# 42 instead of 32 tokens in the second gathered set of a PEER layer

## The chip, the core and the metric

The kernel runs on one core of a Trainium2 chip. The metric is device time in microseconds; the kernel before took 2982.0 us (median of three runs, 2977.97 to 2984.56). "MB" and "GB/s" are decimal.

## What is computed

One decoder layer in float32 on 512 tokens of width 2048: RMSNorm, one input projection, two mixers side by side (a chunked gMLP and an mLSTM), an output projection, and then the part that this change touches, a product-key expert retrieval (PEER), followed by a last RMSNorm.

```python
qp = (xc @ peer_wq).reshape(128, 8, 128)          # per token 8 heads
s1, s2 = q1 . peer_k1, q2 . peer_k2               # 128 scores each
v1, i1 = top_k(s1, 16);  v2, i2 = top_k(s2, 16)
cand = v1[:, None] + v2[None, :]                  # 256 candidates
sv, pos = top_k(cand, 16);  eidx = i1*128 + i2 at pos
gate = softmax(sv)
u_sel, v_sel = peer_u[eidx], peer_v[eidx]         # (128 tokens, 8, 16, 2048)
act = gelu(einsum("td,thkd->thk", xc, u_sel))
y   = einsum("thk,thkd->td", gate * act, v_sel)
```

Each token picks 128 of 16384 experts (8 heads, 16 each); a row of `peer_u` or `peer_v` is 8 KB, a table 134 MB.

## The kernel before

**Two ways for the experts.** The tokens are shared between two ways that run at the same time. *Gathered* tokens (the first `TG` = 160): an indirect DMA on GpSimd's queue (L553) fetches 128 rows of a table, one expert row for each partition, 1 MB at a time; VectorE multiplies a `peer_u` row by the token's input and sums (L580), or adds a gated `peer_v` row to an accumulator (L594). The first set is tokens 0 to 127, one token per partition, 128 fetches for each table. The second set is `G2` = 32 tokens, of which each stands on `S2` = 4 partitions with 32 experts each, so it takes 32 fetches for each table, and at the end a small matmul (`pick`, L885 to L890) adds up the four partial sums. Its input rows `h21` must stand four times on the partitions; L578 reads them from DRAM with an outermost dimension of 4 copies and a step of 0.

*Dense* tokens (`TD` = 352): TensorE computes every expert for them. All of `peer_u` and `peer_v` is streamed in 1 MB loads on SyncE's queue (`raw`, L91), each split into a high and a low float32r half (`split`: ScalarE L73 makes `whi`, VectorE L74 makes `wlo`), and each product is three matmuls (`mm3`, L102 to L104). One *piece* is half a load: 24 matmuls of 352 columns. 256 pieces make the `pu` loop (L742) and 256 the `pv` loop (L835). Between the two, expert activations go to DRAM as `Ad` (L758), and the gates, scattered by one-hot matmuls (`combine`, L668: `pwb`), as `Wd`, in blocks of 32 tokens. `product(g)` (L709) loads both for eight experts (`At`, `Wt`), multiplies them on VectorE (L721) and splits the result (`C`), which is the moving operand of the `pv` matmuls.

**What sets the order.** Python generators interleave the streams, and a scheduler then orders each engine's queue. After each piece `gather_step` (L627) issues `left/slots` gathers, (2·128 + 2·32)/466 = 0.69 for each piece, at a share of 0.45 around the change of loops (once `product(0)` has begun, and in the first 12 pieces of `pv`); a gather is tied to the matmuls of the pieces just before it (`pace`, L555), so that TensorE's pace sets the gathers' pace. Routing (`route`, 102 steps, taken as 1.15 each) and `combine` (88 steps) are spread over the pieces of `pu` by the rate at L764, and `product(0)` begins when they have ended. Weight loads run three pieces ahead. All of VectorE's work stands in one queue in order: splits, gathered rows, routing, PSUM evacuations (L853) and products, so a VectorE instruction that waits holds up the splits behind it, and with them TensorE.

**The end.** `settle` (L808) transposes the dense result back, adds the residual rows `xf` (loaded at L895, one DMA for each of the pieces of tokens in `toks`: 96, 128 and 128 rows), normalizes, and stores `out` in six DMAs (L832), two for each of the three.

Of the kernel before, what the change touches and what calls it, by code (L numbers as in the profile page):

```python
# [39 lines left out]
def layer(ctx, tc, a, out, dbg=None):  # L40
# [440 lines left out]
    def route(t, heads=range(8), nb=4):  # L481
        s = slice(t * P, (t + 1) * P)
        for h0 in range(heads[0], heads[-1] + 1, nb):
# [54 lines left out]
            if t == 1:  # L538
                for q in range(S2):
                    c = q * G2 - r.start  # L540
                    if 0 <= c < nb * TOPK:
                        d = slice(q * G2, (q + 1) * G2)
                        nc.sync.dma_start(eidx2[d, :], ei[0:G2, c:c + G2])
                        nc.sync.dma_start(gate2[d, :], sels[t][0:G2, 2, d])
                        done[1] += 1
# [119 lines left out]
    NB = TD // 32  # L665
    Wd = tc.dram_tile([NB, P, P, 32], F32, name="Wd")

    def combine():  # L668
# [3 lines left out]
        with ExitStack() as wx:  # L672
# [3 lines left out]
            for t in range(1, NT):  # L676
# [5 lines left out]
                for blk in range(G2 // 32 if t == 1 else 0, 4):  # L682
                    wst = wp.tile([P, P, 32], F32, name="wst", bufs=2)
                    for f in range(8):
                        pw = bank("sm", f"pwb{t}_{blk}_{f}")
                        c0 = blk * 32 + f * 4
                        four = [P, 4, P]
                        o1 = wp.tile(four, F32, name="o1", bufs=2)
                        o2 = wp.tile(four, F32, name="o2", bufs=2)
                        nc.vector.tensor_tensor(o1, io[:, None, :].to_broadcast(four),  # L690
                                                sT[:, 0, c0:c0 + 4, None].to_broadcast(four), op=ALU.is_equal)
                        nc.vector.tensor_tensor(o2, io[:, None, :].to_broadcast(four),
                                                sT[:, 1, c0:c0 + 4, None].to_broadcast(four), op=ALU.is_equal)
                        for i in range(4):
                            nc.scalar.activation(o1[:, i, :], o1[:, i, :], AF.Copy, scale=sT[:, 2, c0 + i:c0 + i + 1])
                            nc.tensor.matmul(pw[:, i * P:(i + 1) * P], o2[:, i, :], o1[:, i, :], start=True, stop=True)  # L696
                        nc.scalar.activation(wst[:, :, f * 4:f * 4 + 4].rearrange("p i t -> p t i"),
                                             pw.rearrange("p (t i) -> p t i", t=4), AF.Copy)
                        yield
                    nc.gpsimd.dma_start(Wd[(t - 1) * 4 + blk - G2 // 32], wst)  # L700
# [258 lines left out]
```

## Time and profile before

| | us |
|---|---|
| median of 3 runs | 2982.0 |
| the profiled execution | 2980.37 |
| its span (first to last instruction) | 2978.7 |
| TensorE busy (matmul) | 2893.9 (97%) |
| VectorE busy | 2195.9 (74%) |
| ScalarE busy | 1131.2 (38%) |
| GpSimd busy | 543.1 (18%) |
| granted TensorE clock, mean | 0.988 |
| DMA | 800.76 MB, mean 269 GB/s |

An average over the whole span hides the stages: the first 818 us (the mixers) move little data, and from 900 us on weights, gathered rows and products share the DMA engines. So the rows below are read by stage. "PE" is TensorE, "DVE" VectorE, "ACT" ScalarE, "POOL" GpSimd, "SP" SyncE; a "q" behind an engine's name is its queue. A matmul's duration in a row is not its price: the matmuls overlap, and the distance from start to start counts.

### The profile page before, as it was taken

The numbers are of one execution on the slowest core, as the hardware profiler recorded it, in microseconds if no ns is written. First come the engines' busy times: TensorE is split into PE (matmuls) and PEld (weight loads), VectorE is DVE, ScalarE is ACT, GpSimd is POOL, SyncE is SP. The second block draws the span as 40 slices with busy tenths as digits, with TensorE's granted clock in tenths as the row PEclk, the third lists the DMA queues.
The fourth block names the chain that finished last, engine by engine and source line by source line (L and its number), as shares of the span: only waits on it lengthen the run. The fifth ranks groups of instructions, "written<-read, shape, count | busy, mean of one in ns | idle before, by whom it ended". The sixth has DMA issues, their size and how long they took to land.

```text
span 2978.7 us, 41459 instructions
## 1 busy us (share of the span) xinstructions
PE 2893.9 (97%) x16709; PEld 2727.6 (92%) x16709; DVE 2195.9 (74%) x3026; ACT 1131.2 (38%) x1634; POOL 543.1 (18%) x363
## 2 busy tenths in 40 slices
PE   9999999999989999999999999979999999999997
PEld 7888888887889999999999999979999999999997
DVE  5634333324598999998888886668988989889955
ACT  5322244323243333334676675322323333232233
POOL 0000000000022313322122221013323332223200
PEclk9999999999999999999999999989999999999999
DMA  6223222324379888989889889889999999999853
GB/s 241 85 85 121 85 92 92 106 93 178 112 285 360 312 319 307 330 328 347 305 342 367 332 330 356 315 260 357 370 365 360 361 368 355 362 367 352 344 198 108
DMA packets 147029, 800.76 MB, mean 269 GB/s; under 512 B 15108, under 2 KB 37684, under 8 KB 68596
## 3 DMA queue, kind: packets, MB, share of 16 engines
q1 hardware_dynamic: 87604, 401.68, 36.7%
q0 software_dynamic: 50016, 373.36, 33.3%
q10 hardware_dynamic: 9216, 23.07, 2.0%
q8 instruction: 131, 2.15, 0.3%
q14 instruction: 62, 0.51, 0.0%
HBM read 741.39 MB, written 56.62 MB: 268 GB/s over the span
## 4 chain that ended last, share of the span: by engine, by line
PE 84%; DVE 7%; DMA 5%; issue 2%; ACT 1%; SPq 0%; ACTq 0%; DVEq 0%; POOLq 0%
PE pv L104 9%; PE pu L104 9%; PE pu L102 9%; PE pu L103 9%; PE pv L102 9%; PE pv L103 9%; PE pn L102 4%; PE pn L103 4%; PE pn L104 4%; PE pwb L696 3%; DMA raw<-in_v 2%; DVE wlo L74 2%; PE po L102 2%; PE po L104 2%; PE po L103 2%
## 5 line engine op out<-in xcount | busy, mean ns | idle before, releaser
L73 ACT ACTIVATE whi<-raw 128x1024 fp32r<-128x1024 f32 x642 | 664.7, 1056 | 1395.5 <-DMA raw<-in_v 435.2
L74 DVE TENSOR_TENSOR wlo<-raw,whi 128x1024 fp32r<-128x1024 f32 x642 | 773.1, 1217 | 494.8 <-ACT whi L73 491.0
L102 PE MATMUL pu<-Th,whi 128*128 128x352 f32 x2048 | 671.4, 328 | 13.7 <-ACT whi L73 13.7
L102 PE MATMUL pv<-C,whi 128*128 128x352 f32 x2048 | 663.0, 324 | 18.4 <-ACT whi L73 18.3
L104 PE MATMUL pu<-Th,wlo 128*128 128x352 f32 x2048 | 664.8, 326 | 9.6 <-DVE wlo L74 9.5
L103 PE MATMUL pu<-Tl,whi 128*128 128x352 f32 x2048 | 664.0, 324 | 0.0
L103 PE MATMUL pv<-C,whi 128*128 128x352 f32 x2048 | 661.9, 324 | 0.0
L104 PE MATMUL pv<-C,wlo 128*128 128x352 f32 x2048 | 607.2, 325 | 13.1 <-DVE wlo L74 13.1
L553 POOL DMA_INDIRECT g<-in_peer_v,eidx x160 | 274.7, 1717 | 745.3 <-PE pv L104 303.1
L102 PEld LDWEIGHTS pv<-C,whi 128*128 128x128 f32 x2048 | 386.5, 189 | 21.0 <-ACT whi L73 19.9
L102 PEld LDWEIGHTS pu<-Th,whi 128*128 128x128 f32 x2048 | 388.0, 189 | 16.3 <-ACT whi L73 15.7
L104 PEld LDWEIGHTS pu<-Th,wlo 128*128 128x128 f32 x2048 | 387.1, 189 | 11.4 <-DVE wlo L74 11.0
L104 PEld LDWEIGHTS pv<-C,wlo 128*128 128x128 f32 x2048 | 377.1, 189 | 18.8 <-DVE wlo L74 17.9
L580 DVE CUSTOM_DVE_ANT_0 g<-h,g 128x2048 f32<-128x2048 f32 x160 | 364.5, 2281 | 39.2 <-DMA g<-in_peer_u,eidx 39.1
L553 POOL DMA_INDIRECT g<-in_peer_u,eidx x160 | 248.1, 1550 | 793.3 <-PE pu L104 268.9
L594 DVE SCALAR_TENSOR_TENSOR acc<-g,gate,acc 128x2048 f32<-128x2048 f32 x160 | 375.2, 2345 | 18.8 <-DMA g<-in_peer_v,eidx 18.3
L103 PEld LDWEIGHTS pu<-Tl,whi 128*128 128x128 f32 x2048 | 387.7, 189 | 0.1
L103 PEld LDWEIGHTS pv<-C,whi 128*128 128x128 f32 x2048 | 386.2, 189 | 0.8 <-issue 0.8
L103 PE MATMUL pn<-wlo,Th 128*128 128x512 f32 x512 | 204.9, 400 | 0.0
L104 PE MATMUL pn<-whi,Tl 128*128 128x512 f32 x512 | 203.7, 398 | 0.0
L102 PE MATMUL pn<-whi,Th 128*128 128x512 f32 x512 | 182.9, 399 | 0.0
L853 DVE TENSOR_TENSOR top<-pv,top 128x352 f32<-128x352 f32 x240 | 119.5, 517 | 71.6 <-PE pv L104 70.5
(269 smaller groups left out, 2841.8 us busy)
## 6 DMA issues: line engine op xcount, KB each, us to landing
raw<-in_u SPq DMA_DIRECT2D x128, 1024.0 KB, 7.3
raw<-in_v SPq DMA_DIRECT2D x128, 1024.0 KB, 7.4
raw<-in_w_in SPq DMA_DIRECT2D x80, 512.0 KB, 3.3
Ad<-ast ACTq DMA_DIRECT2D x64, 352.0 KB, 6.9
Wd<-wst POOLq DMA_DIRECT2D x11, 2048.0 KB, 13.0
At<-Ad SPq DMA_DIRECT2D x32, 704.0 KB, 8.3
raw<-in_w_out SPq DMA_DIRECT2D x32, 512.0 KB, 3.3
Wt<-Wd SPq DMA_DIRECT2D x32, 512.0 KB, 10.1
```

Of the source, the lines that this page charges most:

```text
L73: nc.scalar.activation(hi, src, AF.Copy)
L74: nc.vector.tensor_tensor(lo, src, hi.bitcast(F32), op=ALU.subtract)
L102: nc.tensor.matmul(o, sh, mh, start=start, stop=False)
L103: nc.tensor.matmul(o, sh, ml, start=False, stop=False)
L104: return nc.tensor.matmul(o, sl, mh, start=False, stop=stop)
L553: i = nc.gpsimd.indirect_dma_start(out=g, out_offset=None, in_=table, in_offset=bass.IndirectOffsetOnAxis(ap=ix[:, q:q + 1], axis=0))
L580: nc.vector.tensor_tensor_reduce(out=g, in0=h[n], in1=g, op0=ALU.mult, op1=ALU.add, scale=1.0, scalar=0.0, accum_out=act[:, q:q + 1])
L594: nc.vector.scalar_tensor_tensor(acc[n], g, gt[:, q:q + 1], acc[n], op0=ALU.mult, op1=ALU.add)
L696: nc.tensor.matmul(pw[:, i * P:(i + 1) * P], o2[:, i, :], o1[:, i, :], start=True, stop=True)
L853: nc.vector.tensor_tensor(o, po[db], o, op=ALU.add)
```

## The change

`G2` becomes 42, so each token of the second set stands on `S2` = 3 partitions (126 of 128 are used), with 43, 43 and 42 experts: `Q2` = 43 fetches for each table, 342 gathers in all instead of 320. `TD` becomes 342, which is no multiple of 32: `combine` walks the tokens in chunks of up to 4 (88 steps as before, five of them with 2 tokens), and the 22 tokens behind the ten blocks go to a buffer of their own, `Wl`, with a load and a multiply of their own in each `product`. The rate at L764 is computed from `NB` = 10 instead of 11. The input rows of the second set are written three times to `h2d[1]` in the early part (42, 42, 42 and 2 rows, four stores on GpSimd's queue instead of one), and read later with one plain load of 128 rows. The first piece of dense tokens has 86 rows instead of 96.

```diff
-G2 = 32
+G2 = 42
 S2 = P // G2
+R2 = S2 * G2
+Q2 = -(-P // S2)
 TG = P + G2
 TD = T - TG
...
-            nc.gpsimd.dma_start(h2d[t], hn)
+            for r in range(0, P, P if t == 0 else G2):
+                n = min(P if t == 0 else G2, P - r)
+                nc.gpsimd.dma_start(h2d[t, r:r + n, :], hn[0:n, :])
...
-    eidx2 = hg.tile([P, G2], I32, name="eidx2")
-    gate2 = hg.tile([P, G2], F32, name="gate2")
+    eidx2 = hg.tile([P, Q2], I32, name="eidx2")
+    gate2 = hg.tile([P, Q2], F32, name="gate2")
+    nc.gpsimd.memset(eidx2, 0)
+    nc.gpsimd.memset(gate2, 0.0)
...
-                    rep = bass.AP(tensor=h2d.tensor, offset=h2d[1].offset, ap=[[0, S2], [D, G2], [1, D]])
-                    nc.sync.dma_start(h[1], rep)
+                    nc.sync.dma_start(h[1], h2d[1])
...
-    gathers = {"left": 2 * P + 2 * G2, "slots": NP - 2 + NPC + nv - 24 - 28, "owed": 0.0}
+    gathers = {"left": 2 * P + 2 * Q2, "slots": NP - 2 + NPC + nv - 24 - 28, "owed": 0.0}
...
-    NB = TD // 32
+    NB, TL = TD // 32, TD % 32
     Wd = tc.dram_tile([NB, P, P, 32], F32, name="Wd")
+    Wl = tc.dram_tile([P, P, TL], F32, name="Wl")
...
-                for blk in range(G2 // 32 if t == 1 else 0, 4):
-                    wst = wp.tile([P, P, 32], F32, name="wst", bufs=2)
-                    for f in range(8):
...
+                c0 = max(0, TG - t * P)
+                while c0 < P:
+                    at = t * P + c0 - TG
+                    blk, f = at // 32, at % 32
+                    bw = min(32, TD - blk * 32)
+                    w = min(4, P - c0, bw - f)
...
+                    if f + w == bw:
+                        nc.gpsimd.dma_start(Wd[blk] if bw == 32 else Wl, wst)
+                    c0 += w
+                    yield
...
-            nc.sync.dma_start(w[:, b:b1], Wd[b:b1, :, g * GE:(g + 1) * GE, :].rearrange("b p i t -> p b i t"))
+            nc.sync.dma_start(wf[:, b:b1], Wd[b:b1, :, g * GE:(g + 1) * GE, :].rearrange("b p i t -> p b i t"))
+            if b1 == NB:
+                nc.sync.dma_start(wl, Wl[:, g * GE:(g + 1) * GE, :])
             yield
...
-            av = A[:, s].rearrange("p j (b t) -> p j b t", t=32)
-            nc.vector.tensor_tensor(av, av, w[:, :, s].rearrange("p b j t -> p j b t"), op=ALU.mult)
+            av = A[:, s, 0:NB * 32].rearrange("p j (b t) -> p j b t", t=32)
+            nc.vector.tensor_tensor(av, av, wf[:, :, s].rearrange("p b j t -> p j b t"), op=ALU.mult)
+            nc.vector.tensor_tensor(A[:, s, NB * 32:], A[:, s, NB * 32:], wl[:, s], op=ALU.mult)
```

Three places show how instructions move. The first is SyncE's queue around the change of loops, before, from the first `At` load: `raw` are weight loads, `At` and `Wt` the operands of a product, `top` the last norm's gain, `h` the second set's input rows.

```order
L712 DMA At_15136<-Ad_5433 128x1408 x2
L716 DMA Wt_15137<-Wd 128x4x256 x2
L716 DMA Wt_15137<-Wd 128x3x256
L91 DMA raw<-in_u 128x2048 x2
L716 DMA Wt_15137<-Wd 128x4x256 x2
L716 DMA Wt_15137<-Wd 128x3x256
L712 DMA At_15136<-Ad_5434 128x1408 x2
L91 DMA raw<-in_u 128x2048 x2
L716 DMA Wt_15137<-Wd 128x4x256 x2
L716 DMA Wt_15137<-Wd 128x3x256
L91 DMA raw<-in_u 128x2048 x3
L91 DMA raw<-in_v 128x2048 x3
```

The same place in the changed kernel, from its first `At` load; 35 `raw` loads of `in_u` stand in one row ahead of it (25 before).

```order
L726 DMA At_15417<-Ad_5439 128x1368 x2
L730 DMA Wt_15418<-Wd 128x4x256 x2
L730 DMA Wt_15418<-Wd 128x2x256
L732 DMA Wt_15418<-Wl 128x176
L93 DMA raw<-in_u 128x2048 x2
L730 DMA Wt_15418<-Wd 128x4x256 x2
L730 DMA Wt_15418<-Wd 128x2x256
L732 DMA Wt_15418<-Wl 128x176
L726 DMA At_15417<-Ad_5440 128x1368 x2
L93 DMA raw<-in_u 128x2048
L93 DMA raw<-in_v 128x2048
L730 DMA Wt_15418<-Wd 128x4x256 x2
```

Before, seven weight loads of `in_u` stand behind the first `At` load; in the changed kernel three. The second place follows on the same queue (in the changed kernel two more `raw` loads of `in_v` and two `Wt` rows lie between): before, from the gain on.

```order
L787 DMA top<-in_final_g 128x2048
L91 DMA raw<-in_v 128x2048
L712 DMA At_15136<-Ad_5435 128x1408 x2
L579 DMA h_20571<-h2d 128x1x2048
L91 DMA raw<-in_v 128x2048
L716 DMA Wt_15137<-Wd 128x4x256 x2
L716 DMA Wt_15137<-Wd 128x3x256
L91 DMA raw<-in_v 128x2048 x6
```

And in the changed kernel:

```order
L804 DMA top<-in_final_g 128x2048
L726 DMA At_15417<-Ad_5441 128x1368 x2
L93 DMA raw<-in_v 128x2048 x2
L583 DMA h_19666<-h2d 128x2048
L730 DMA Wt_15418<-Wd 128x4x256 x2
L730 DMA Wt_15418<-Wd 128x2x256
L732 DMA Wt_15418<-Wl 128x176
L93 DMA raw<-in_v 128x2048 x5
```

The load of `h` has lost its copy dimension and stands behind two weight loads instead of one; from the first `At` load of the first place to the last `Wt` row of this one, eight weight loads are left of the twelve that stood between them. The third place is the end of SyncE's queue, before:

```order
L91 DMA raw<-in_v 128x2048 x17
L895 DMA xf_23967<-x2d 96x2048
L895 DMA xf_23968<-x2d 128x2048
L895 DMA xf_23969<-x2d 128x2048
L803 DMA out<-acc_22133 32x2048
L91 DMA raw<-in_v 128x2048 x4
L832 DMA out<-xf_23967 96x1024 x2
L832 DMA out<-xf_23968 128x1024 x2
L832 DMA out<-xf_23969 128x1024 x2
```

And in the changed kernel:

```order
L93 DMA raw<-in_v 128x2048 x17
L913 DMA xf_24067<-x2d 86x2048
L913 DMA xf_24068<-x2d 128x2048
L913 DMA xf_24069<-x2d 128x2048
L820 DMA out<-acc_21679 42x2048
L93 DMA raw<-in_v 128x2048 x4
L849 DMA out<-xf_24067 86x1024 x2
L849 DMA out<-xf_24068 128x1024 x2
L849 DMA out<-xf_24069 128x1024 x2
```

The order is the same; the first load and the first two stores have 86 rows where they had 96, and the second set's store 42 where it had 32.

## Rows read from the trace of the kernel before

**Rows 1.** Busy time by stage: columns in the first line (x: instructions; clock; DMA)

```profile
core 0: us, PE busy (x) PEld busy (x) DVE busy (x) ACT busy (x) POOL busy (x), PEclk, DMA share, GB/s
900.00:975.00 75.00, 75.00 (x470) 74.95 (x469) 63.36 (x94) 23.61 (x31) 17.74 (x14) 1.00 0.93 357
975.00:1350.00 375.00, 361.33 (x2210) 356.99 (x2208) 371.24 (x787) 131.57 (x173) 101.69 (x62) 0.99 0.88 321
1350.00:1825.00 475.00, 473.31 (x3169) 473.22 (x3169) 397.44 (x406) 313.50 (x598) 112.61 (x81) 1.00 0.89 338
1825.00:2000.00 175.00, 157.06 (x955) 155.73 (x954) 102.02 (x78) 53.19 (x59) 18.64 (x16) 0.94 0.87 300
2000.00:2825.00 825.00, 809.24 (x5010) 803.54 (x5009) 740.06 (x653) 251.34 (x242) 250.41 (x144) 1.00 0.94 360
2825.00:2960.00 135.00, 135.00 (x836) 130.98 (x835) 79.45 (x97) 45.09 (x58) 3.90 (x2) 1.00 0.43 156
```

**Rows 2.** TensorE's timeline at 930 us: start us, us, engine, line, operation

```profile
930.00 0.32 PE L102 MATMUL pu<-Th,whi 128*128 128x352 f32 x1
...
934.96 0.32 PE L103 MATMUL pu<-Tl,whi 128*128 128x352 f32 x1
```

**Rows 3.** TensorE's timeline at 350 us, 512 columns

```profile
352.66 0.40 PE L103 MATMUL pn<-wlo,Th 128*128 128x512 f32 x1
...
355.94 0.40 PE L102 MATMUL pn<-whi,Th 128*128 128x512 f32 x1
```

**Rows 4.** VectorE's groups, 975 to 1350 us: busy us, mean ns, idle before

```profile
L580 DVE CUSTOM_DVE_ANT_0 g<-h,g 128x2048 f32<-128x2048 f32 x63 | 143.3, 2276 | 3.0 <-DMA g<-in_peer_u,eidx 3.0
L74 DVE TENSOR_TENSOR wlo<-raw,whi 128x1024 fp32r<-128x1024 f32 x90 | 107.1, 1209 | 0.8 <-ACT whi L73 0.8
```

**Rows 5.** VectorE's groups, 2000 to 2825 us

```profile
L594 DVE SCALAR_TENSOR_TENSOR acc<-g,gate,acc 128x2048 f32<-128x2048 f32 x112 | 262.5, 2344 | 11.1 <-DMA g<-in_peer_v,eidx 10.8
L74 DVE TENSOR_TENSOR wlo<-raw,whi 128x1024 fp32r<-128x1024 f32 x207 | 246.9, 1216 | 20.9 <-ACT whi L73 17.9 <-PE pv L104 2.8
...
L580 DVE CUSTOM_DVE_ANT_0 g<-h,g 128x2048 f32<-128x2048 f32 x32 | 72.8, 2283 | 1.1 <-DMA g<-in_peer_u,eidx 1.1
...
L721 DVE TENSOR_TENSOR At<-At,Wt 128x1408 f32<-128x1408 f32 x26 | 42.0, 1615 | 0.0
```

**Rows 6.** Three stretches of high traffic, columns as in group 1

```profile
2200.00:2300.00 100.00, 99.89 (x623) 99.31 (x622) 90.19 (x75) 27.10 (x26) 32.76 (x18) 1.00 0.97 373
2625.00:2650.00 25.00, 25.00 (x158) 25.00 (x157) 23.58 (x27) 10.80 (x10) 6.47 (x5) 1.00 0.98 385
1984.00:1988.00 4.00, 4.00 (x27) 4.00 (x26) 4.00 (x3) 1.06 (x1) 0.00 (x0) 1.00 1.06 424
```

**Rows 7.** SyncE's timeline at 1937 us

```profile
1937.49 0.68 SPq L579 DMA_DIRECT2D h<-h2d  x1
```

**Rows 8.** Chain of waits, 1940 to 1975 us: start us, us, what

```profile
1940.21 31.54 DMA raw<-in_v
...
1974.23 0.66 PE pv L104
1974.89 0.29 PE pv L102
```

**Rows 9.** 4 us stretches of the stall, columns as in group 1

```profile
1956.00:1960.00 4.00, 1.50 (x10) 1.21 (x8) 0.00 (x0) 0.00 (x0) 0.00 (x0) 1.00 1.16 229
1964.00:1968.00 4.00, 0.00 (x0) 0.00 (x0) 0.00 (x0) 0.00 (x0) 0.00 (x0) 0.50 0.28 105
```

**Rows 10.** SyncE's timeline from 2964 us to the end

```profile
2967.86 5.54 SPq L832 DMA_DIRECT2D out<-xf  x6
```

**Rows 11.** DMA issues from 2960 us: count, KB each, median us to landing

```profile
out<-xf SPq DMA_DIRECT2D x4, 512.0 KB, 5.3
out<-xf SPq DMA_DIRECT2D x2, 384.0 KB, 3.8
```

**Rows 12.** DMA issues, 2892 to 2908 us

```profile
xf<-x2d SPq DMA_DIRECT2D x1, 768.0 KB, 8.2
```

More of the change, by code (lines that the diff above doesn't have):

```diff
@@ L539, in route @@
                 for q in range(S2):
[L540 to L545, printed above, removed]
+                    lo, hi = max(q * Q2, r.start), min((q + 1) * Q2, r.stop)
+                    if lo < hi:
+                        d, f = slice(q * G2, (q + 1) * G2), slice(lo - q * Q2, hi - q * Q2)
+                        nc.sync.dma_start(eidx2[d, f], ei[0:G2, lo - r.start:hi - r.start])
+                        nc.sync.dma_start(gate2[d, f], sels[t][0:G2, 2, lo:hi])
+                done[1] = r.stop
             yield
@@ L564, in experts @@
     def experts():
-        sets = ((eidx, gate0, P), (eidx2, gate2, G2))
+        sets = ((eidx, gate0, P), (eidx2, gate2, Q2))
         h = [h20, None]
@@ L569, in ready @@
         def ready(n, q):
-            return done[0] > q if n == 0 else done[1] >= S2
+            return done[0] > q if n == 0 else done[1] >= P
         def consume(n, table, q, g):
-            nq = sets[n][2]
-            gt = sets[n][1]
+            gt, nq = sets[n][1:]
             if table == 0:
@@ L681, in combine @@
                 nc.scalar.activation(sT, pt[:, 0:384].rearrange("p (n t) -> p n t", n=3), AF.Copy)
-                for blk in range(G2 // 32 if t == 1 else 0, 4):
-                    wst = wp.tile([P, P, 32], F32, name="wst", bufs=2)
-                    for f in range(8):
[L685 to L700, printed above, removed]
@@ new lines, in combine @@
+                c0 = max(0, TG - t * P)
[4 more added lines that the diff above has]
+                    w = min(4, P - c0, bw - f)
+                    if f == 0:
+                        wst = wp.tile([P, P * 32], F32, name="wst", bufs=2)[:, 0:P * bw].rearrange(
+                            "p (i t) -> p i t", t=bw)
+                    pw = bank("sm", f"pwb{t}_{c0}")[:, 0:w * P]
+                    four = [P, w, P]
+                    o1 = wp.tile([P, 4, P], F32, name="o1", bufs=2)[:, 0:w, :]
+                    o2 = wp.tile([P, 4, P], F32, name="o2", bufs=2)[:, 0:w, :]
+                    nc.vector.tensor_tensor(o1, io[:, None, :].to_broadcast(four),
+                                            sT[:, 0, c0:c0 + w, None].to_broadcast(four), op=ALU.is_equal)
+                    nc.vector.tensor_tensor(o2, io[:, None, :].to_broadcast(four),
+                                            sT[:, 1, c0:c0 + w, None].to_broadcast(four), op=ALU.is_equal)
+                    for i in range(w):
+                        nc.scalar.activation(o1[:, i, :], o1[:, i, :], AF.Copy, scale=sT[:, 2, c0 + i:c0 + i + 1])
+                        nc.tensor.matmul(pw[:, i * P:(i + 1) * P], o2[:, i, :], o1[:, i, :], start=True, stop=True)
+                    nc.scalar.activation(wst[:, :, f:f + w].rearrange("p i t -> p t i"),
+                                         pw.rearrange("p (t i) -> p t i", t=w), AF.Copy)
+                    if f + w == bw:
+                        nc.gpsimd.dma_start(Wd[blk] if bw == 32 else Wl, wst)
+                    c0 += w
+                    yield
@@ L888, in layer @@
                 ph = bank(("mm", "sm")[ch % 2], f"ph{ch}")
-                nc.tensor.matmul(ph[0:G2, :], pick, y[:, d], start=True, stop=True)
+                nc.tensor.matmul(ph[0:G2, :], pick[0:R2, :], y[0:R2, d], start=True, stop=True)
                 nc.scalar.activation(y[0:G2, d], ph[0:G2, :], AF.Copy)
```

7 lines of the change are left out of this document (5 added, 2 removed).

## The prediction

> **What bounds the kernel now.** I read first the busy time by stage, then TensorE's timeline for the price of a matmul, then VectorE's groups, the DMA rates, and the chain of waits where TensorE stands still. In the table by stage [rows 1] the reader is to see that TensorE is the bound nearly everywhere from 900 us on, but that its shadow changes. Dividing the matmuls by 24 gives the pieces. From 975 to 1350 us (2210 less 43 small ones: 90.3 pieces) VectorE is busy for 371.2 of 375 us and a piece takes 4.15 us; from 1350 to 1825 us (3169 less 698 small ones: 103 pieces) TensorE is busy for 473.3 of 475; from 2000 to 2825 us (208.7 pieces, 3.953 us each) TensorE loses some 3% while the DMA engines show 0.94 and 360 GB/s. The rest: 19.6 pieces from 900, 39.2 from 1825, 33 from 2825 us.
>
> Price of a matmul: 31 starts lie between the two rows at 930 us, 4.96 us, so 160.0 ns for 352 columns [rows 2]; 14 starts cover 3.28 us at 512 columns, 234 ns [rows 3]; both are close to 0.456 ns for a column. A piece of 24 at full speed is 3.84 us. So from 2000 us TensorE loses 825 − 208.7 × 3.84 = 24 us.
>
> One stop is of another kind. SyncE issues the load of `h` at 1937.49 [rows 7]; the weight load behind it, issued at 1940.21, takes 31.54 us, and TensorE resumes at 1974.23, at 0.29 us a matmul for 16 rows of which one stands [rows 8]. It had stopped 1.50 us into the stretch from 1956 [rows 9]: 16.7 us lost, and 16 × 0.13 = 2.1 more at the lower clock level (granted 0.50, so 1.2 GHz, in the idle stretch from 1964). In that stretch the DMA engines move only 105 GB/s at a share of 0.28 [rows 9], against 424 with all sixteen [rows 6]: 26.5 GB/s an engine, hence four engines. The load of `h` has an outermost dimension of 4 copies.
>
> **The change part by part.** The sum goes against the profiled execution, 2980.4 us, which lies 1.6 us under the median.
>
> *Ten columns less.* 12288 matmuls go from 160.0 to 155.5 ns if the price stays in proportion; by the difference of the two rows (74 ns for 160 columns) it is the same. The other end is nothing, if the weight loads set the step, which also fill their row of the table (PEld is busy as long as PE [rows 1]). But such a floor would not grow with the columns as the two steps do, so I take −0.109 us a piece where TensorE sets the pace: −2.1 us from 900, −11.2 from 1350, −4.3 from 1825, −3.6 from 2825 us. The stretch from 1350 would then move 338 GB/s × 4.61 us = 1.56 MB a piece, +0.04 with the gathers, in 4.50 us: 355 GB/s, below what the later stage holds. VectorE is at 84% there. 20 fewer one-hot matmuls are left uncounted.
>
> *22 more gathers.* 22/466 = 0.047 a piece, each 1.05 MB and 2.28 to 2.34 us of VectorE [rows 4, 5]: +0.11 us. From 975 to 1350 us VectorE has no room (4.11 us a piece). The lower rate at the loop (197.3/205.3) takes 4% of the routing from each piece: VectorE's 371 us less 107 of splits and 143 of gathered rows leave 1.3 us a piece, so −0.05. That makes 4.17 of work, 4.21 at the same 99%: +5 us, and 4% more pieces at this pace rather than TensorE's, +2. Together +7, and no gain from the columns; bounds 0 (the slower routing opens gaps) and +12 (no relief from the routing).
>
> From 2000 us VectorE goes from 3.55 to 3.66 us a piece; the extra multiply of 22 tokens (two for each 16 pieces, at the least 1615 ns × 88/1408 = 0.10) adds under 0.03. That lies beside TensorE's 3.73 and is covered, if barely. The DMA engines: 360 GB/s × 3.953 = 1.423 MB a piece; +0.0495 for the gathers, −0.005 for the smaller products: 1.467. At TensorE's new pace this needs 393 GB/s. Before, full pace needed 370, and the best 100 us gave 373 with TensorE almost unbroken; the best 25 us 385 [rows 6]. So this stage becomes bound by transfers. At the rate of before, 360, a piece takes 4.075 us, +25 us over 208.7 pieces; at 385 it takes 3.81, −30. More demand fills more of the gaps, so I take 372, next to the best 100 us: 3.944, −2 us.
>
> *The load of `h`.* One contiguous load of 128 rows goes on all engines; the stop of 18.8 us goes. Next late is the burst around it: eight weight loads now lie between the first `At` and the last `Wt` row instead of twelve. Three `At` and four `Wt` sets of 1.40 MB, 8.4 MB of weights, 2.1 for the gain and `h`, about 5.5 of gathers at the reduced share and 1.4 of `Ad` stores are 27.2 MB, for which TensorE leaves 16 × 3.73 = 59.7 us. At 372 GB/s they take 73, at 424 64 us: a stop of 4 to 13, of which three pieces of prefetched weights (11 us) can hide all. Bounds 0 and +13, taken +7. The early copy is three more stores on GpSimd's queue; queued behind them are the loads of the first set's inputs and of the routing keys, and who waits for those is the routing, which needs the whole query projection first: 0, at most a few us.
>
> *The end.* The last six stores are issued from 2967.86 us [rows 10] and land a median of 3.8 and 5.3 us later [rows 11]: 2.88 MB at 424 GB/s is 6.8 us, so all engines work. Loads of 96 and 128 rows split evenly over sixteen; 4 copies got four. 86 = 2 × 43 splits evenly over two or one. The trace has no such store. Bounds: nothing, if it is spread anyway; 26.6 + 4.9 − 6.8 = +25 on one engine. Two engines: each carries half of 704.5 KB and its sixteenth of the other 2.10 MB, 483 KB at 26.5 GB/s, 18.2 us instead of 6.8: +11, which I take, as the row with 4 engines is nearest. By the Trainium skill ("DMA: Bandwidth & Descriptors", "Why a DMA increments its semaphore by 16 and not by 1") a DMA runs on the largest number of engines up to 16 that divides the slowest dimension of both sides; that would be 4 for the old `h`, with which the 105 GB/s agree, and 2 for 86 rows. The `xf` load of 86 rows, 8.2 us before [rows 12], would take 13.3 and more, but is used four pieces later with three pieces of splits ahead: 0, at most +5.
>
> Sum: −2.1 + 7 − 11.2 − 4.3 − 18.8 + 7 − 2 − 3.6 + 11 = −17.0. The profiled execution would be 2963, the median 2965 us.
>
> **Rivals.**
>
> *A. The transfers do not go above 360 GB/s.* Then the stage from 2000 us costs +25.5 instead of −2 and the burst 27.2/0.360 = 75.6, so +16 instead of +7: 3001 us, slower. It decides from below about 365 GB/s, where that stage alone eats the other gains (1.467/0.365 = 4.02 us, +14). For it: 0.94 busy, and weight loads late at each product. Against it: 373 held for 100 us, 385 for 25. The Trainium skill ("DMA: Bandwidth & Descriptors", "Where 436 GB/s comes from") has HBM bind at about 358 GB/s for a core; by that, 4.10 us a piece. The rows above it say that one core alone is not held there.
>
> *B. The 86 rows are spread over all engines.* No +11: 2954. For it nothing but that no such store is in the trace.
>
> *C. The transfers follow to 385 GB/s.* −30 instead of −2: 2937. For it the 25 us rows, in which TensorE was unbroken; against it that these are peaks between product loads.
>
> *D. A new stop takes the place of the old one at the change of loops,* since VectorE waits in its queue for the third and fourth `Wt` set and the splits wait behind it: the 18.8 us come back, 2984. For it the compressed queue; against it that the old stop came from four engines alone.
>
> **How the numbers follow.** Forecast 0.45, A 0.19, B 0.12, C 0.10, D 0.14. A change below 0.2% (6 us) can't be told from none. B and C are faster, most of the forecast (its own range is 2950 to 2980) and a part of D; A and a part of D are slower: faster 0.60, same 0.18, slower 0.22. The range goes from near C's 2937 to near A's 3001: 2941 to 2996.
>
> **What would show it.** The steps of TensorE's rows: 155 to 156 ns. No stop with a weight load of 30 us near the load of `h`; instead short waits for `Wt`. VectorE at 99% from 975 to 1350 us with about 4.2 us a piece. From 2000 us about 3.94 us a piece at 370 GB/s or more; 360 or less is A. The last stores landing up to 20 us after their issue, with a DMA share near 2/16 in the last microseconds; a share near 1 is B. It is wrong if the columns do not shorten the step, or if VectorE, not the transfers, is what the pieces wait for in the later stage.

## The result and the profile after

The changed kernel takes 3007.1 us (median of 8 runs, 2992.5 to 3017.0) against 2981.7 for the kernel before: ratio 1.0083, 95% interval 1.006 to 1.0105, 25 us slower. 2965 had been forecast. The profiled execution took 2992.5, the fastest of the eight; a second profile (e5 below) has a span of 2996.6.

The pieces are the better ruler here than fixed times: the start of piece 0, 128 and 224 of the `pu` loop, and of 16 and 224 of the `pv` loop, bound five stretches, and the last matmul a sixth. Worked out from the starts of the matmuls in the profiled executions, in us; the last column counts, in the order of the instructions, the places on ScalarE where no piece is split ahead (explained with e13):

| kernel | 0-128 | 128-224 | to `pv` 16 | 16-224 | to last matmul | end | none ahead |
|---|---|---|---|---|---|---|---|
| before | 530.8 | 442.7 | 214.8 | 822.4 | 131.3 | 18.0 | 1 |
| after | 546.8 | 443.2 | 197.6 | 826.8 | 133.9 | 29.8 | 14 |
| e5, after again | 547.3 | 442.6 | 198.4 | 829.6 | 131.5 | 29.7 | 14 |
| e1, before + early copy | 528.6 | 443.1 | 196.5 | 822.7 | 131.3 | 18.0 | 1 |
| e3, 64 fetches | 532.4 | 426.9 | 197.8 | 820.5 | 132.7 | 30.2 | 4 |
| e9, 342 fetches, 320 row operations | 534.2 | 443.7 | 196.9 | 829.3 | 133.6 | 29.8 | 15 |
| e10, 320 fetches, 342 row operations | 546.8 | 424.8 | 194.7 | 832.4 | 132.8 | 29.8 | 6 |
| e6, Gelu tied | 545.4 | 440.2 | 203.1 | 844.1 | 130.5 | 29.7 | 8 |
| e13, Gelu and combining tied | 543.5 | 416.2 | 204.2 | 823.7 | 132.4 | 29.6 | 0 |
| e14, e13 + rows cut | 545.0 | 416.2 | 204.3 | 829.2 | 128.7 | 18.4 | 0 |

The busy times of the changed kernel in the first five stretches (the fifth with the end; columns as in [rows 1]):

```profile
core 0: us, PE busy (x) PEld busy (x) DVE busy (x) ACT busy (x) POOL busy (x), PEclk, DMA share, GB/s
812.90:1359.70 546.80, 504.02 (x3146) 496.32 (x3144) 538.47 (x1124) 195.80 (x262) 197.38 (x96) 0.97 0.87 323
1359.70:1802.80 443.10, 429.40 (x2865) 425.29 (x2865) 357.42 (x346) 262.73 (x496) 129.97 (x79) 0.98 0.90 340
1802.80:2000.40 197.60, 192.34 (x1259) 191.51 (x1258) 149.08 (x131) 90.32 (x134) 42.94 (x28) 0.99 0.93 363
2000.40:2827.20 826.80, 797.87 (x4995) 786.04 (x4994) 761.43 (x699) 248.27 (x240) 241.70 (x151) 1.00 0.96 369
2827.20:2990.80 163.60, 132.58 (x825) 127.47 (x824) 77.35 (x122) 50.60 (x69) 0.00 (x0) 0.91 0.36 127
```

Before, the first two were:

```profile
818.70:1349.60 530.90, 509.62 (x3120) 505.15 (x3119) 513.50 (x1090) 187.82 (x242) 141.76 (x88) 0.98 0.87 321
1349.60:1792.20 442.60, 440.91 (x2950) 440.58 (x2949) 370.16 (x381) 291.05 (x553) 106.70 (x76) 1.00 0.89 337
```

In the first row VectorE is full, as it was from 975 us in [rows 1]. The second row is the odd one: TensorE, idle for less than 2 us of it before, now stands for 14 of 443 us, though VectorE is at 81% and the DMA engines at 0.90.

The step of a matmul, which answers to [rows 2] (TensorE's timeline; rows between left out): 20 steps in 3.06 us, 153 ns.

```profile
929.84 0.32 PE L104 MATMUL pu<-Th,whi 128*128 128x342 f32 x1
...
932.90 0.32 PE L106 MATMUL pu<-Th,wlo 128*128 128x342 f32 x1
```

In the `pv` loop, where the moving operand is `C`, 22 steps take 3.45 us, 157 ns:

```profile
2299.92 0.32 PE L104 MATMUL pv<-C,whi 128*128 128x342 f32 x1
...
2303.37 0.32 PE L104 MATMUL pv<-C,whi 128*128 128x342 f32 x1
```

From `pv` 16 to 224 TensorE stands for 29 us, before for 16. Most of it is waits for `wlo` (us, times, longest):

```profile
PE pv L106 <- DVE wlo L76: 21.6, 31, 2.1
```

and before:

```profile
PE pv L104 <- DVE wlo L74: 12.8, 11, 2.2
```

Around the load of `h` (issued at 1951.85 us) TensorE does not stop any more, which answers to [rows 8, 9]:

```profile
1950.00:1975.00 25.00, 25.00 (x161) 25.00 (x160) 19.60 (x23) 6.15 (x6) 2.36 (x3) 1.00 0.98 389
1975.00:2000.00 25.00, 25.00 (x162) 25.00 (x161) 19.21 (x17) 7.50 (x7) 7.41 (x5) 1.00 0.79 307
```

The end, which answers to [rows 10, 11]; the last store is issued at 2974.07 us:

```profile
2970.00:2980.00 10.00, 0.00 (x0) 0.00 (x0) 0.00 (x0) 0.68 (x1) 0.00 (x0) 0.50 0.62 231
2980.00:2990.00 10.00, 0.00 (x0) 0.00 (x0) 0.00 (x0) 0.00 (x0) 0.00 (x0) 0.50 0.12 47
```

In the last 10 us the share is 0.12, two engines of sixteen, at 47 GB/s: the 86 rows. By the Trainium skill ("DMA: Bandwidth & Descriptors", "Why a DMA increments its semaphore by 16 and not by 1") 86 rows get two engines, since 2 is the largest number up to 16 that divides them; the trace agrees.

And one stop of the second stretch, on ScalarE first (start us, duration, engine, line, operation; in brackets the idle time ahead and what ended it):

```profile
1573.67 1.23 ACT L705 ACTIVATE o<-o,selT 128x128 f32<-128x128 f32 x4
1580.38 0.46 ACT L772 ACTIVATE ast<-pu 128x342 f32<-128x342 f32 x1 [5.49 <-PE pu L106]
1580.87 0.33 ACTq L775 DMA_DIRECT2D Ad<-ast  x1
1581.24 1.95 ACT L707 ACTIVATE wst<-pwb 128x512 f32<-128x512 f32 x2 [0.40 <-PE pwb L706]
1583.00 1.24 ACT L705 ACTIVATE o<-o,selT 128x128 f32<-128x128 f32 x4
1584.14 1.99 ACT L75 ACTIVATE whi<-raw 128x1024 fp32r<-128x1024 f32 x2
1586.03 1.26 ACT L705 ACTIVATE o<-o,selT 128x128 f32<-128x128 f32 x4
1587.20 1.07 ACT L707 ACTIVATE wst<-pwb 128x512 f32<-128x512 f32 x1
1588.07 2.00 ACT L75 ACTIVATE whi<-raw 128x1024 fp32r<-128x1024 f32 x2
```

and on TensorE in the same time:

```profile
1580.03 0.32 PE L106 MATMUL pu<-Th,wlo 128*128 128x342 f32 x1
1580.19 1.72 PE L706 MATMUL pwb<-o,o 128*128 128x128 f32 x14
1583.41 1.37 PE L706 MATMUL pwb<-o,o 128*128 128x128 f32 x8 [1.50 <-ACT o L705]
1585.23 0.42 PE L104 MATMUL pu<-Th,whi 128*128 128x342 f32 x1 [0.46 <-ACT whi L75]
1585.49 0.32 PE L105 MATMUL pu<-Tl,whi 128*128 128x342 f32 x1
1586.47 2.07 PE L706 MATMUL pwb<-o,o 128*128 128x128 f32 x8 [0.66 <-DVE o L700]
1589.18 0.65 PE L104 MATMUL pu<-Th,whi 128*128 128x342 f32 x1 [0.63 <-ACT whi L75]
```

ScalarE stands idle for 5.5 us at the Gelu (`ast`), which waits for TensorE to finish the piece; behind it in its queue stand two `wst`, which wait for TensorE too, four `o`, and only then the `whi` that TensorE needs next. TensorE has finished its split pieces at 1580.19; until 1589.18 it has only matmuls of the combining and two of `pu`, with gaps between them. Its waits in the whole stretch are 13.7 us; the two longest are both for ScalarE, for an `o` that stands behind such an operation or for the `whi` itself:

```profile
PE pwb L706 <- ACT o L705: 5.5, 6, 1.5
PE pu L104 <- ACT whi L75: 3.7, 5, 2.0
```

A stop costs more than it lasts. Behind this one the granted clock is 0.50, which is the level of 1.2 GHz:

```profile
1588.00:1592.00 4.00, 3.37 (x13) 3.07 (x13) 4.00 (x6) 4.00 (x8) 4.00 (x1) 0.50 0.37 105
```

Over the stretch the mean granted clock is 0.98, where it was 1.00 before; 2% of 443 us is some 9 us, an estimate, on top of the 14. Such stops lie at 1461, 1580, 1660, 1700 and 1779 us, and 2 to 5 us later in the second profile. The waits of ScalarE in the stretch (us, times, longest) say it in sum: it waits 140.8 us to do the Gelu and 2.4 for a weight load to land. The weights are not late.

```profile
ACT ast L772 <- PE pu L106: 140.8, 42, 6.9
ACT whi L75 <- DMA raw<-in_u: 2.4, 2, 1.2
```

Before, the same two were (1349.6 to 1792.2 us):

```profile
ACT whi L73 <- DMA raw<-in_u: 23.3, 8, 5.2
...
ACT ast L755 <- PE pu L104: 4.1, 3, 2.1
```

### The profile page after: what moved, and what is told of

It reads as the page before. It is cut to its first block, busy times and chain, and to the rows that moved or that the text cites. A ratio compares the mean times of both kernels' runs of the same rounds, so it can differ in the third digit from the quotient of the medians.

```text
span 2990.8 us, 41516 instructions
## 1 busy us (share of the span) xinstructions
PE 2857.3 (96%) x16689; PEld 2677.9 (90%) x16689; DVE 2239.0 (75%) x3091; ACT 1122.1 (38%) x1624; POOL 629.4 (21%) x390
## 4 chain that ended last, share of the span: by engine, by line
PE 67%; DVE 19%; DMA 7%; issue 5%; ACT 1%; SPq 0%; ACTq 0%; DVEq 0%; POOL 0%; POOLq 0%
PE pu L106 7%; PE pu L104 7%; PE pu L105 7%; PE pv L106 6%; DVE wlo L76 6%; PE pv L104 6%; PE pv L105 6%; DVE g L584 5%; PE pn L104 4%; PE pn L105 4%; PE pn L106 4%; DMA raw<-in_v 3%; PE pwb L706 2%; DVE acc L598 2%; PE po L104 2%
## 5 line engine op out<-in xcount | busy, mean ns | idle before, releaser
L104 PE MATMUL pu<-Th,whi 128*128 128x342 f32 x2048 | 661.7, 323 | 30.8 <-ACT whi L75 29.7
L106 PE MATMUL pu<-Th,wlo 128*128 128x342 f32 x2048 | 659.3, 323 | 22.1 <-DVE wlo L76 22.1
L104 PE MATMUL pv<-C,whi 128*128 128x342 f32 x2048 | 655.6, 321 | 7.6 <-ACT whi L75 7.6
L105 PE MATMUL pu<-Tl,whi 128*128 128x342 f32 x2048 | 654.6, 320 | 0.0
L105 PE MATMUL pv<-C,whi 128*128 128x342 f32 x2048 | 652.7, 320 | 0.0
L106 PE MATMUL pv<-C,wlo 128*128 128x342 f32 x2048 | 576.4, 321 | 22.4 <-DVE wlo L76 22.3
L559 POOL DMA_INDIRECT g<-in_peer_u,eidx x171 | 312.2, 1826 | 727.0 <-PE pu L106 236.5
L559 POOL DMA_INDIRECT g<-in_peer_v,eidx x171 | 295.1, 1726 | 726.8 <-PE pv L106 243.7
L598 DVE SCALAR_TENSOR_TENSOR acc<-g,gate,acc 128x2048 f32<-128x2048 f32 x171 | 401.7, 2349 | 26.2 <-DMA g<-in_peer_v,eidx 24.8
L584 DVE CUSTOM_DVE_ANT_0 g<-h,g 128x2048 f32<-128x2048 f32 x171 | 395.6, 2321 | 28.8 <-DMA g<-in_peer_u,eidx 28.7
L772 ACT ACTIVATE ast<-pu 128x342 f32<-128x342 f32 x128 | 57.7, 451 | 285.1 <-PE pu L106 284.9
```

The lines of the kernel that those rows point to most:

```text
L104: nc.tensor.matmul(o, sh, mh, start=start, stop=False)
L105: nc.tensor.matmul(o, sh, ml, start=False, stop=False)
L106: return nc.tensor.matmul(o, sl, mh, start=False, stop=stop)
L559: i = nc.gpsimd.indirect_dma_start(out=g, out_offset=None, in_=table, in_offset=bass.IndirectOffsetOnAxis(ap=ix[:, q:q + 1], axis=0))
L584: nc.vector.tensor_tensor_reduce(out=g, in0=h[n], in1=g, op0=ALU.mult, op1=ALU.add, scale=1.0, scalar=0.0, accum_out=act[:, q:q + 1])
L598: nc.vector.scalar_tensor_tensor(acc[n], g, gt[:, q:q + 1], acc[n], op0=ALU.mult, op1=ALU.add)
```

## The experiments

Ratios are to the kernel before on the same chip; for the changed kernel they were 1.0083 and 1.008, so 0.001 is 3 us.

**e1: the early copy alone**, in the kernel before.

```
-            nc.gpsimd.dma_start(h2d[t], hn)
+            for r in range(0, P, P if t == 0 else G2):
+                n = min(P if t == 0 else G2, P - r)
+                nc.gpsimd.dma_start(h2d[t, r:r + n, :], hn[0:n, :])
...
-                    nc.sync.dma_start(h[1], rep)
+                    nc.sync.dma_start(h[1], h2d[1])
```

> The kernel before, with only the early part of the change: the 32 input rows of the second set are written four times to DRAM, and `h` is loaded as 128 plain rows. Theory 1 (the stop at the load of `h` was a plain loss of 18.8 us, and its removal is a gain that the changed kernel also got, hidden under other losses): 2962 to 2967 us, ratio 0.994 to 0.995, no idle stretch of TensorE near 1957 to 1974 us. Rival (the stop only moved work: transfers and gathers that caught up during the stop are now late elsewhere): above 2975 us, ratio above 0.998.

Measured 2963.3 us, 0.9948 (0.9928 to 0.9968). The stretch around the change of loops falls from 214.8 to 196.5 us and nothing is given back. Theory 1 holds: the stop was a plain loss.

**e2: the rate of the combining** with the units that it has.

```
-            owed_c += (102 * HEAVY + 8 * NB) / (NPC - 24 - started)
+            owed_c += (102 * HEAVY + 88) / (NPC - 24 - started)
```

> The changed kernel, with 88 instead of 8 x NB = 80 units in the rate at which routing and combining are spread over the loop (88 is the number of units that it has). Theory 1 (the pieces lose because VectorE and the DMA engines have 7% more gathers to do; where the units stand matters little): 3000 to 3012 us, as the changed kernel. Rival (the rate of 80 ends the combining late, so the first product and its loads are pressed into fewer pieces at the change of loops, the 5 us that pieces 208 to 255 lost in the trace): 2995 to 3002 us, the pieces from 208 back to 206 us, the first product's loads about 40 us earlier.

Measured 3000.6 us, 1.0071 (1.0051 to 1.009): at most a few us. The stretch to `pv` 16 did not get shorter (201.9).

**e3: 32 fetches for each table**; the other 11 columns of experts are left out.

```
-        sets = ((eidx, gate0, P), (eidx2, gate2, Q2))
+        sets = ((eidx, gate0, P), (eidx2, gate2, 32))
...
-    gathers = {"left": 2 * P + 2 * Q2, ...
+    gathers = {"left": 2 * P + 64, ...
```

> The changed kernel with 32 instead of 43 fetches for each table in the second set; it leaves out the experts of 11 of the 43 columns, so 22 gathers of 1 MB with their row operations on VectorE. Everything else stays: 342 dense columns, 86-row stores, the rate of 80 units. Theory 1 (the 22 gathers eat the gain of the columns): about 22 x 1.05 MB / 370 GB/s = 62 us less of transfers and 22 x 2.3 = 51 us less of VectorE; where these set the pace that comes back: 2955 to 2970 us, and the loop of the first table 10 to 18 us shorter. Rival (the loss is in the sizes 342 and 86, the rate, and the end): less than 10 us comes back, 2997 or more.

Measured 2962.8 us, 0.9946 (0.9928 to 0.9964). 41 us come back with the 22 gathers, by the profile 14.4 in pieces 0 to 128 and 16.3 in 128 to 224. So the loss hangs on the gathers; in which way, this run does not tell.

**e4: the 86 rows cut**, loads and stores; the edit of the stores is shown, that of the loads is the same.

```
+                cut = 80 if rows == TD % P else rows
+                for p0, p1 in ((0, cut), (cut, rows)):
+                    if p0 < p1:
+                        nc.sync.dma_start(out[t0 + p0:t0 + p1, s], xf[j][p0:p1, s])
```

> The changed kernel, with the loads of `xf` and the last stores of the 86 rows each cut in two, 80 and 6 rows. Theory (86 = 2 x 43 rows go on two engines, and the end waits 11.7 us for them): the last matmul to the end of the span falls from 29.7 to 18 or 19 us, the time by 10 to 12 us, to 2994 to 2998 us. Rival (the end is long because the last stores follow a later start or another wait, not because of the row count): no change, 3005 to 3009 us.

Measured 2980.2 us, 1.0013 (0.9998 to 1.0028): 21 us. In the profile the end takes 18.0 instead of 29.8 us, as the theory has it. The eight stores, issued from 2962.64 us, are done at 2973.5; most of the bytes pass in this stretch, and no 10 us with two engines follow:

```profile
2960.00:2970.00 10.00, 0.00 (x0) 0.00 (x0) 4.18 (x25) 3.76 (x6) 0.00 (x0) 0.60 0.64 231
```

**e5: the changed kernel again.**

> The changed kernel once more, beside the next three on the same chip, with a second profile. If its slowness is in the order of its work: about 3005 us (2998 to 3012) and the same stops of TensorE near the same places (1461, 1580, 1660, 1700, 1779 us), 14 us or so longer from piece 128 to 208 of the first loop than with 32 fetches for each table. If the 10 to 15 us by which the profiled execution was faster than the median are in one stage, a slower profile shows which.

Measured 3005.6 us, 1.008 (1.006 to 1.01). The stretches repeat within 3 us and the stops at their places.

**e6: the Gelu tied behind the splits.** A dependency on the `whi` of the next two pieces, on the same engine.

```
+            gelu = nc.scalar.activation(ast[:, e % 2, :], pu, AF.Gelu_apprx_tanh)
+            for hi, lo in queue[0:2]:
+                tc.add_manual_dep(gelu.ins, act_of[id(hi)].name, ...
```

> The changed kernel, with the Gelu of each pair of pieces tied behind the splits of the next two pieces on ScalarE, on which it comes next anyway; no work is added or taken. In the trace of the changed kernel the Gelu stands ahead of those splits at 11 places from about 1460 us on, and TensorE ran out of split weights there. Theory 2 (a good part of the cost of the 22 gathers is that they upset the order on ScalarE: the Gelu waits for its matmuls while the next weights wait behind it): the stops of 3 to 5 us at 1461, 1580, 1660, 1700 and 1779 us go, pieces 128 to 208 take 350 to 356 us instead of 365, and the time falls by 12 to 25 us, to 2982 to 2995 us. Rival, theory 1 (the gathers' work on VectorE and the DMA engines sets the pace, and the order only shows where it is paid): the stops come at other instructions, pieces 128 to 208 stay at 361 us or more, 3000 to 3010 us.

Measured 2999.7 us, 1.0068 (1.0043 to 1.0093). Only the stop at 1660 us went; at the others the `wst` now stood first. Theory 2 in this form failed, and was too narrow: the Gelu is not the only operation on ScalarE that waits for TensorE. **e8**, the same with the rows cut, took 2985.8 us, 1.0016 (1.0 to 1.0032), no better than e4.

**e7: 16 tokens.**

```
-G2 = 42
+G2 = 16
```

> The code of the changed kernel with 16 tokens in the second set: eight groups of 16, 16 fetches for each table (27 fewer for each table than with 42), 368 dense columns (26 more), 112 rows in the place of the 86. If the balance found with 32 against 43 fetches holds further (41 us for 22 gathers, so 1.9 us a gather, against some 2 us for a column): 2982 to 2963 less 60 for 32 gathers more than made up by 16 columns at 2 us, 32: about 2935 us, against 2963 for 32 tokens with the early copy. Rival (with so few gathers TensorE sets the pace everywhere, and a column costs all of 12288 x 0.456 ns = 5.6 us): 2963 + 16 x 5.6 - 0 to 60, so 2993 to 3050 us, slower than before.

Measured 3017.3 us, 1.0117 (1.0099 to 1.0135), inside the rival's range. In pieces 128 to 224 the 16 columns more than in e1 are paid in full: 462.3 us against 443.1, and 96 × 24 steps at 168 instead of 160 ns are 18.4. In pieces 0 to 128 they are not (533.8 against 528.6). The end takes 18.5 us with its 112 rows, seven times sixteen. So the 2 us a column of the expectation was no price to go on.

**e9 and e10: VectorE or the transfers.** e9 keeps the 342 fetches and leaves out 22 row operations; e10 keeps the operations, 22 of them on a tile that is already there, and leaves out 22 fetches. Part of the edit of e9 is shown.

```
+        def skip(n, q):
+            return q % 16 == 15 or (n == 1 and q == Q2 - 1)
...
-            nc.vector.scalar_tensor_tensor(acc[n], g, gt[:, q:q + 1], acc[n], op0=ALU.mult, op1=ALU.add)
+            if not skip(n, q):
+                nc.vector.scalar_tensor_tensor(acc[n], g, gt[:, q:q + 1], acc[n], op0=ALU.mult, op1=ALU.add)
```

> The changed kernel with all its 342 gathers, but without VectorE's operation on every sixteenth gathered tile (and on the last of each table in the second set): 22 operations of 2.3 us are left out, spread over both loops. Theory 1a (the 22 gathers cost mostly through VectorE's in-order queue: 6 more of them in the routing stretch are 14 us, and the rest delays the splits and one-hots behind them): most of the 41 us that fewer fetches gave back comes back, 2965 to 2980 us, pieces 0 to 128 of the first loop 532 to 535 us instead of 547. Rival, theory 1b (the transfers are the price): 2995 us or more, and the first loop as long as before the cut.

> The counterpart: 320 gathers instead of 342, but all 342 operations of VectorE; in the place of every sixteenth gathered tile (and the last of each table in the second set) the operation reads a tile that is already there, so that part of the experts is left out. Theory 1a (VectorE): little comes back, 2995 to 3007 us. Theory 1b (transfers): 22 x 1.05 MB less, most of the 41 us comes back, 2963 to 2980 us; in the second loop from 2000 to 2800 us the pieces go from 3.97 to 3.95 us or less either way.

Measured: e9 2999.8 us, 1.0079 (1.0066 to 1.0092); e10 2976.2 us, 0.9992 (0.9979 to 1.0005). The first two stretches of e9, then of e10:

```profile
814.50:1348.80 534.30, 500.05 (x3126) 488.95 (x3125) 525.94 (x1110) 189.42 (x251) 161.09 (x95) 0.98 0.88 330
1348.80:1792.40 443.60, 429.50 (x2871) 425.51 (x2870) 349.06 (x339) 264.63 (x499) 113.35 (x78) 0.98 0.89 342
```

```profile
813.00:1359.80 546.80, 501.68 (x3132) 490.60 (x3130) 539.40 (x1123) 193.79 (x258) 148.95 (x89) 0.98 0.84 313
1359.80:1784.50 424.70, 420.00 (x2860) 418.27 (x2859) 354.20 (x341) 263.87 (x489) 100.03 (x75) 1.00 0.91 346
```

The stretches answer in opposite ways. Pieces 0 to 128 are VectorE's: without the operations 534 us, without the transfers 547, as in the changed kernel. Pieces 128 to 224 do not care for the operations. It looked as if transfers were the price there; but the order of the instructions is another in each kernel, and e10 has 6 places with nothing split ahead against 15 of e9. That is why e13 was made.

**e11 and e12: the gathers shifted** from pieces 0 to 119 to 120 to 207, in e1's kernel and in e4's.

```
-        gather_step(last, 1.0 if begun is None else 0.45)
+        gather_step(last, 0.45 if begun is not None else 0.85 if n < 120 else 1.2 if n < 208 else 1.0)
```

> The kernel before with the early copy, and the gathers of the first loop shifted: a share of 0.85 for the pieces 0 to 119 and 1.2 for 120 to 207, so some 12 gathers move from the stretch in which VectorE is full to the one in which it is at 83%. If a gather in the routing stretch costs its whole 2.3 us of VectorE and one in the combining stretch little: 12 x 2.3 = 28 us less for pieces 0 to 128, at most 5 to 10 us given back behind, 2938 to 2955 us. Rival (the gathers stall TensorE wherever they are put, as the stops of the changed kernel in the combining stretch suggest): 2958 to 2970 us.

> The changed kernel with the 86 rows cut into 80 and 6 and the same shift of the gathers (0.85, then 1.2). If the shift gains in the routing stretch and the combining stretch has room: 2955 to 2970 us instead of 2980. If the combining stretch is already where the 7% more gathers stop TensorE: pieces 128 to 208 grow by what pieces 0 to 128 gain, 2975 to 2990 us.

e11: 2996.1 us, 1.0063 (1.005 to 1.0076), 33 us worse than e1. Pieces 0 to 128 gain 8.1 us (some 12 gathers fewer, 28 expected), the next stretch loses 8.9, that to `pv` 16 19.4, and `pv` 16 to 224 16.4. Neither the expectation nor its rival held. Its order has 12 places with nothing split ahead, e1's has one. e12: 2984.2 us, 1.0014 (1.0002 to 1.0027), as e4; 23 us gained in pieces 0 to 128 are lost by `pv` 16, behind the stretch that the expectation named.

**e13: all that waits on ScalarE tied.** As e6, and the combining's `o` and `wst` tied as well; no work added or left out.

```
+        tie[:] = [act_of[id(w[0])] for w in queue[0:2]]
...
-                        nc.scalar.activation(o1[:, i, :], ...
+                        behind(nc.scalar.activation(o1[:, i, :], ...
...
-                    nc.scalar.activation(wst[:, :, f:f + w]...
+                    behind(nc.scalar.activation(wst[:, :, f:f + w]...
```

> The changed kernel with all its gathers; on ScalarE the Gelu and the operations of the combining (`o`, `wst`) are tied behind the splits of the next two pieces. No work is added or taken. Theory O (the order on ScalarE: TensorE runs out of split weights because operations that wait for TensorE itself stand ahead of the splits): pieces 128 to 224 take 425 to 430 us instead of 443, the stops of 3 to 5 us at 1461, 1580, 1700 and 1779 us go, the time falls to 2985 to 2993 us. Theory T (the transfers of the 7% more gathers: weights land late whatever the order): pieces 128 to 224 stay at 438 us or more, with waits for `raw`, 3000 us or more.

Measured 2978.0 us, 0.9994 (0.9979 to 1.0009): 26 to 27 us less than the changed kernel. The stretch from 128 to 224, and ScalarE's waits in it:

```profile
1359.40:1775.60 416.20, 416.05 (x2856) 415.57 (x2855) 348.98 (x339) 265.20 (x493) 125.10 (x78) 1.00 0.94 362
```

```profile
ACT ast L784 <- PE pu L116: 55.5, 27, 5.0
...
ACT whi L82 <- DMA raw<-in_u: 6.2, 6, 2.2
```

TensorE is busy for all but 0.15 us, with all gathers, at 362 GB/s instead of 340, and at a granted clock of 1.00. Theory O holds, T falls: the transfers had room. Some 4 units of the combining more than in the changed kernel lie in the next stretch (140 rows of `pwb` on TensorE against 104, eight for a unit), which is 6 us longer. The count in the table's last column is of Gelus and `wst` on ScalarE for which no piece beyond TensorE's own is split ahead of them in the order of the instructions. Before there is one such place, and three or four pieces are split ahead of 86 of the 88 `wst`; after: 8 Gelus and 6 `wst`; in e6 8 `wst`; in e13 none. Among the kernels of 342 columns in the table the stretch from 128 to 224 goes with the count: 416 us at none, 425 to 427 at 4 and 6 (e3 and e10, which also do less work), 440 to 444 at 8 to 15.

**e14: e13 and e4 together.**

> As the run before, and the 86 rows cut into 80 and 6. Theory O: 2980 less 12 to 18 us, 2962 to 2970 us, as fast as the kernel before with the early copy. Theory T: 2976 to 2986 us, as with the cut alone.

Measured 2958.8 us, 0.993 (0.9911 to 0.9948): the lowest ratio of the study, some 45 us under the changed kernel by the ratios. Its interval overlaps that of e1: that the 42 tokens gain anything beyond the early copy alone is not shown.

**e15: the stores of `wst` on ScalarE's queue.**

```
-                        nc.gpsimd.dma_start(Wd[blk] if bw == 32 else Wl, wst)
+                        nc.scalar.dma_start(Wd[blk] if bw == 32 else Wl, wst)
```

> The changed kernel with the stores of `wst` issued from ScalarE's queue, which makes `wst`, instead of GpSimd's, where the gathers behind them wait. Theory Q (the gathers come late and in bunches because they stand behind these stores): GpSimd's waits of 8 to 16 us before a gather go and pieces 128 to 224 fall to 425 to 435 us, 2987 to 2997 us. Theories O and T: no change within 6 us, 3000 to 3010 us.

Measured 3006.6 us, 1.0088 (1.0068 to 1.0108). Theory Q falls: the stores on GpSimd's queue are not the cause.

**e16 and e17: stores or load alone** of e4's cut.

> The changed kernel with only the last stores of the 86 rows cut into 80 and 6. If the stores are the whole of it: 12 to 20 us less, 2986 to 2995 us, the time from the last matmul to the end 18 us. If the load of `xf` costs as well: 12 us at most, 2993 to 2996 us, and the next run gains the rest.

> The changed kernel with only the load of `xf` of the 86 rows cut into 80 and 6. If the stores are the whole of it: no change, 3000 to 3010 us. If the load costs as well (it lands late, and the splits of the last pieces or the last sums wait): 6 to 9 us less, 2997 to 3001 us.

Measured 2987.0 us, 1.0021 (1.0007 to 1.0036), and 2991.0 us, 1.0033 (1.0018 to 1.0047). In the profiles the stores are worth 12 us (end 29.8 to 17.7) and the load 2 to 5: with the load cut the stretch to the last matmul is 128.7 us in all five profiles of 42 tokens, otherwise 130.5 to 134.2. VectorE waits for it in the changed kernel:

```profile
DVE xf L834 <- DMA xf<-x2d: 8.7, 3, 5.3
```

So both cost. The medians give 18 and 14 us apart and 20 to 21 together, which is more than the profiles explain, and for the load more than either form of the expectation; this stays open.

**e18: the tie in e1's kernel**, whose order is good.

> The kernel before with the early copy, and the Gelu and the combining's operations tied behind the splits of the next two pieces, as in e13. If the tie gains only where the order was upset: 2960 to 2967 us, as without it, pieces 128 to 224 at 443 us. Rival (it gains in any kernel): 2950 us or less.

Measured 2966.7 us, 0.996 (0.9946 to 0.9973); pieces 128 to 224 take 444.0 us. The tie gains nothing where the order was not upset.

## Why the prediction was wrong

By the second profile the forecast's steps stand as follows; the first differs by at most 3 us a stretch.

- *The columns.* Right in kind: the step fell from 160 ns to 153 in the `pu` loop, below the 155.5 forecast, but only to 157 in the `pv` loop.
- *From 1350 us, −11.2: the step that failed.* Measured 0 (442.6 against 442.7). The argument was that the stretch needs 355 GB/s and VectorE has room; both were true, as e13 shows with 362 GB/s and 416.2 us, a gain of 26.5 (96 pieces × 24 × 6.5 ns = 15.0, and 12 fewer units of combining in the stretch, at some 0.8 us of TensorE each, by the rows of before from 1502.90 us). In the changed kernel the stops, 14 us, and the lower clock behind them, some 9, took these gains back. What failed is what was not looked at: the order on ScalarE. Costs were added as work by engine; but ScalarE takes its queue in order, and the rows show 5 us at a Gelu that waits for TensorE, with TensorE's next weights behind it. No rival had it. It could be read from the order of the instructions without a run.
- *The routing stretch, +5 with its columns.* Measured 16.5. The mechanism is right (VectorE full; e9 takes 13 us off), the size is not: 6 more gathers in it are 13.8 us at 2.3, and the relief of 4% from a slower routing, taken as −0.05 us a piece, turned round. In the second profile more of the routing and the combining lies before piece 128 than in the kernel before: 48 operations on `oh` (51.7 us of VectorE) instead of 41 (43.2 us), and 5.0 us of `o` where there was none. VectorE's busy time went from 513.5 to 539.5 us; some 9.5 us of it filled idle time, and 16.5 made the stretch longer. Why the order brought this work forward is open.
- *The load of `h`, −18.8 + 7 − 4.3 = −16.1.* Right: −16.4 in the second profile, −17.2 in the first, and −18.3 alone in e1. Rival D did not happen.
- *From 2000 us, −2 at 372 GB/s.* Measured +4 to +7 at 369 GB/s. The transfers went where they were forecast, above 360; neither A (held at 360) nor C (385 throughout) happened. The Trainium skill's limit of about 358 GB/s ("DMA: Bandwidth & Descriptors", "Where 436 GB/s comes from"), which stands beside A, does not agree with this trace, in which one core moved 369 GB/s for 827 us. The forecast's 1.467 MB a piece make 3.976 us at 369 GB/s instead of 3.944 at 372, which is 6.6 us over the 208 pieces. But that the transfers set the time is not shown: TensorE's waits here end mostly with VectorE, which the prediction had named as a sign against it (21.6 us for `wlo`, before 12.8). Nor is it shown that VectorE sets it: e9 and e10 both took longer here than e3, with either half of the work gone, and with all of it e2 took 819 us and e6 844. What bounds this stretch is not settled.
- *The end, +11 − 3.6.* The stores: 11.8, right, and rival B falls. The load of `xf`, taken as 0 with a bound of 5, costs 2 to 5, which ate the columns' 3.6.

Sum of the second profile: +16.5 − 0.1 − 16.4 + 7.2 + 0.2 + 11.7 = +19.1, and 1.3 less for the earlier start: +17.8, where −17.0 was forecast. Of the 35 us between them some 11 lie in the stretch from 1350 us, 12 in the routing, 9 from 2000 us and 4 at the load of `xf`. The medians say 25: some 7 us do not show in the profiles, which were the fastest of their runs both times. Some of it may be the clock: of the eight executions the profiled one has a mean granted clock of 0.984, the two slowest (3015 and 3017 us) 0.978 and 0.979, and 0.001 of 3000 us is 3 us. What makes that difference is open.

With the order and the rows repaired (e14) the ratio is 0.993. That e14 took 2959 us, near the 2954 of the forecast without its +11 for the stores, is luck: its first stretch is 14 us longer than before where 5 were forecast, the second 26 shorter where 11 were, and the stretch from `pv` 16 on 7 longer where it should have been 2 shorter. Why the scheduler of the program put the waiting operations first once the gathers had changed was not tried.

## What to carry to other kernels

Before summing work by engine, read each in-order queue for what stands ahead of the operations that feed the bound engine: an operation that waits for that engine, placed ahead of its next input, costs a stop whatever the busy shares say, and here time at the lower clock behind it. When a size changes and a scheduler sets the order, compare the order as well as the work, and compare experiments that change the work only after looking whether they changed the order too. And give a DMA's outermost dimension a number that sixteen divides: here 86 rows went on two engines, and cutting them into 80 and 6 was worth 0.7% (e4).

## What the runs showed of the hardware

The step of a matmul of the same shape, 342 columns, was 153 ns with `Th` or `Tl` as the moving operand and 157 with `C`; at 352 columns both were 160. The cause was not tried. And one core moved 362 GB/s over 416 us beside a TensorE that stood for 0.15 us of them (e13).
